# A hybrid attention and retention step on one core: the first transfers laid out and placed anew

## The chip, the cores and the metric

One core of one Trainium2 chip runs the whole program, in one launch. The metric is the device time of that launch in microseconds (us), lower is better; it is given as the median of three runs.

## What is computed

Two groups of tokens, a prompt of 1024 and a sample group of 8 (one new token for each of 8 sequences), pass through two layers: sliding-window attention (32 query heads, 4 key heads, window 128, sinks, a relative-position bias) and retention (4 heads, keys of 256, values of 512), each with a SiLU gate, and a last norm. All in 32-bit floats. Cut to what the change touches:

```python
logits = einsum('bqkgd,bskd->bkgqs', q, k) * 64 ** -0.5
bias = rel_bias[t5_bucket(rel)]            # rel = query position - key position
logits = where(valid, logits + bias, -1e30)
m = maximum(max(logits), sink); p = exp(logits - m)
o = einsum('bkgqs,bskd->bqkgd', p / (sum(p) + exp(sink - m)), v)
...
kb = concatenate([cache_k, k_new], axis=1)  # sample group: 128 cached rows and the new one
vb = concatenate([cache_v, v_new], axis=1)
return y, kb[:, 1:], vb[:, 1:]              # the cache moved on by one row
...
q, k = rotary(q, pos), rotary(k, pos)       # retention: cos and sin tables by position
```

## The kernel before

Tokens lie along the free dimension in two halves of 512; the 8 sample tokens ride with the first half, so its width is 520 (`TA`). Nearly all the work is products against weights. Each weight tile is 128 x 512 (256 KB) and is split into a high and a low part, `whi` and `wlo`, so that three products (high by high, high by low, low by high) give nearly full precision. `wload` (L170) does this: SP issues the load into `wraw` (3 buffers), ACT casts it to `whi` (4 buffers), and GpSimd and VectorE take turns to subtract for `wlo` (4 buffers). So a load is issued when the tile three before it has been split, and that needs the buffers of a tile that TensorE has finished. A feature tile of an input projection takes two weight tiles; each weight tile is 24 products of 260 columns (`proj_job`, L347: two column chunks of 12).

The order. Only TensorE's instructions stand in the order in which the code is written (`MANUAL`, L53). Those of the other engines, and the transfers that SP issues, are placed by a scheduler, which estimates times and puts an instruction early where what it needs is there early. Each engine then runs its own list in order. All transfers of the kernel are issued by SP, in one list: when one has to wait, for a buffer, for data, or in its issue, all behind it wait.

The first stretch. The first half's stream is loaded and split as it arrives (`first_x`, L1088), beside the four weight tiles of the value projection (`w_v`, tiles 1 to 4). Then come the two key tiles of features (`k_job`: weight tiles 5 to 8), the first queries (9 to 12) and the first gates (13 to 16), all of `w_in`. `bias_rows` (L441) loads the small tables; after four pieces of the stream (weight tiles 5 and 6) TensorE multiplies the bias table `rb` by the one-hot table `hot` into `bps`, ACT copies this to `brow`, one row of 128 per head, and four transfers (L457) write each row 128 times into DRAM tiles `bdram`. `att_scores` (L608) reads them back with a step of 127 (L613), so that every row is the bias turned by one: one `bias` tile of four heads, a read before each group of four blocks. The first such read stands right behind the four writes.

The attention loop runs 64 slots (L1164): in each slot scores of one tile, turns of the one before, values of the one before that; jobs of the stream are spread between. `extra` hangs further stages on slots: at slot 3 `move_cache` (L709), which moves the sample caches on by one row from DRAM to DRAM, 1016 KB each; at slots 8u + 3, 5 and 7 `att_sample(u)` (L666), the sample group's eight heads: it loads cached keys `kT` (L671), cached values `vc` (L673, rows 1 to 127 on 127 partitions), the new token's value row (L674, from `vsmp` into partition 0), the bias rows `bs` (L679). `load_rope(0)` (L717), hung on slot 56, loads the cos and sin tables that retention reads at L735 and L745. As the scheduler put them, the cache moves, `kT`, `vc` and the rope loads of the first half stand on SP ahead of the sixth weight tile.

Of the kernel before, what the change touches and what calls it, by code (L numbers as in the profile page):

```python
# [10 lines left out]
F32 = mybir.dt.float32  # L11
# [8 lines left out]
P = 128  # L20
# [3 lines left out]
NB = 8  # L24
# [9 lines left out]
# columns of the constant tensor  # L34
# [13 lines left out]
# weight tiles loaded ahead of their use; the slack in spreading the stream, in ns of  # L48
# the tensor engine; products that bring it to its full clock while the first loads come
# [10 lines left out]
class Stream:  # L60
    """The matrix products against the weights, as jobs in their order. A job is a
    generator that yields after each piece with the piece's length on the tensor
    engine; its weight tiles are loaded some tiles ahead of their use."""
# [21 lines left out]
    def step(self):  # L85
        """one piece of the first job; True when the job is over."""
        j = self.jobs[0]
        if j[1] is None:
            j[1] = j[0]()
        try:  # L90
            j[2] -= next(j[1])
            return False
        except StopIteration:
            self.jobs.pop(0)
            return True

    def fill(self, n, goal):
        """the first n jobs until about goal of them is left; how many of them are left."""
# [12 lines left out]
def hybrid_step(ctx: ExitStack, tc: tile.TileContext, I: dict, O: dict):  # L111
# [17 lines left out]
    # ---- token halves: the sample tokens ride with the first half, except in  # L129
    # the last output projection, where they ride with the second  # L130
# [6 lines left out]
    # ---- the residual stream: one half on chip at a time, the other in DRAM  # L137
# [30 lines left out]
    wctr = [0]  # L168

    def wload(src):  # L170
        raw = wp.tile([P, 512], F32, name="wraw", tag="wr", bufs=3)
        sp.dma_start(raw, src)
# [10 lines left out]
    # ================= norms =================  # L183
    H = [None]

    def stats_rows(s, T):
        """the reciprocal root mean squares, with tokens on partitions, from the squares' sums over tiles."""
# [13 lines left out]
    def stats_spread(rs, T, tag):  # L201
        """the same, with tokens along the row, on every partition."""
# [16 lines left out]
    def norm_stats(T, tag, out, stored=None):  # L219
        """out: the reciprocal root mean square of each token, on every partition; in three stages."""  # L220
# [19 lines left out]
    def norm(layer, T, rb_, src):  # L240
        """the normalised half, split in two parts; src(kt, tile) is the stream's tile. In four stages."""
# [32 lines left out]
    def final_norm(hf, T):  # L274
        """in four stages."""
# [8 lines left out]
    def final_part(c0, c1):  # L284
        """the last norm of columns c0..c1 of the second half, in four stages."""
# [54 lines left out]
    # ================= projections =================  # L340
# [6 lines left out]
    def proj_job(src, evac):  # L347
        """one feature tile of an input projection: evac(psum, c0, c1) per column chunk."""
# [18 lines left out]
    def tok_job(srcs, width, smp, evac):  # L367
        """a projection with tokens on partitions: evac(block, psum); block 4 is the
        sample rows, whose two parts lie on partitions 0.. and 32.. and are to be added."""
# [33 lines left out]
    def out_job(T, src, ys, fts):  # L403
        """feature tiles of an output projection, added to the stream."""
# [27 lines left out]
    # ================= attention layer =================  # L432
# [4 lines left out]
    bdram = [dp.tile([8, P, P], F32, name=f"bdram{u}") for u in range(4)]  # L437
# [3 lines left out]
    def bias_rows():  # L441
        """relative-position bias: one row per head, repeated over its period, kept in DRAM."""
# [11 lines left out]
        brow = lp.tile([HEADS, P], F32, name="brow")  # L454
        act.copy(brow, bps[:HEADS, :P])
        for u in range(4):
            sp.dma_start(bdram[u], brow[8 * u : 8 * u + 8, None, :].to_broadcast([8, P, P]))  # L457
            yield
# [82 lines left out]
    def q_jobs(m):  # L541
        """queries of four heads, in the two parts that the tensor engine takes, one above the other."""
# [65 lines left out]
    def att_scores(i):  # L608
        m, b = i // 4, i % 4
        hf, u, t = m // 8, (m // 2) % 4, m % 2  # L610
        if b == 0:
            bi = lp.tile([P, 4, P], F32, name="bias", tag="bias", bufs=2)
            sp.dma_start(bi, bass.AP(bdram[u].tensor, bdram[u].offset + 4 * t * P * P, [[P - 1, P], [P * P, 4], [1, P]]))  # L613
# [731 lines left out]
```

## Time and profile before

| what | value |
|---|---|
| runs | 1785.62, 1788.95, 1789.3 us; median 1788.95 |
| profiled execution, first to last instruction (span) | 1782.7 us |
| what lies around it, against the median (the profiled execution's time is given by its span alone) | 6.25 us |
| TensorE granted clock, mean over the span | 0.981 |
| DMA | 211.30 MB, mean 119 GB/s |
| TensorE waits for its weight tile's first part | 36.1 us, in 2 places |

Times are microseconds from the first instruction. Engines: PE is TensorE, PEld its weight load, DVE is VectorE, ACT ScalarE, POOL GpSimd, SPq the queue of transfers that SyncE issues. A row of a timeline has the start, the length, the engine, the line of the kernel, the operation, what it writes and reads, and in brackets how long the engine had been idle and what released it. For SPq the length is that of the issue, not of the transfer. A row of stretches has, for each engine, its busy time and in brackets how many instructions, then the granted clock (1.00 is full), the busy share of the 16 DMA engines, and GB/s. A row of DMA issues has the number, the size of one, and the median time from issue to landing.

### The profile page before, as it was taken

The page shows a single profiled execution, that of the slowest core. Times are in us where ns is not written, and L with a number is a line of the kernel's source. Part 1 is how long each engine was busy: PE and PEld are TensorE (multiplying, and loading weights), DVE is VectorE, ACT ScalarE, POOL GpSimd, SP SyncE. Part 2 cuts the span into 40 slices and gives each one's busy share as a digit, 9 for nine tenths or more (in the row PEclk, how much of TensorE's full clock was granted, in tenths as well). Part 3 has the DMA queues.
Part 4 walks back from the last instruction along what each step waited for, and adds up shares of the span by engine and source line. Part 5 has one row for each costly group of instructions (what it writes and reads, how often), then busy time and mean ns, then how long its engine had stood idle before and what let it go on. Part 6 is the DMA issues. An engine that isn't in the chain of part 4 may idle for free.

```text
span 1782.7 us, 29003 instructions
## 1 busy us (share of the span) xinstructions
PE 1705.9 (96%) x10550; PEld 1454.3 (82%) x10550; DVE 1049.3 (59%) x2142; ACT 842.2 (47%) x1960; POOL 709.5 (40%) x670
## 2 busy tenths in 40 slices
PE   6489999999999999999999999999999999999997
PEld 6488999898888777778889788787777889888887
DVE  4367767776467666675276465456655655445366
ACT  4255646455555555565354344344443433433344
POOL 2024443445334434344434334234344452443534
PEclk8789999999999999999999999999999999999999
DMA  5432224223234222232366456447454262322323
GB/s 179 81 92 67 89 78 118 85 88 108 88 113 150 83 83 77 77 90 72 107 204 209 144 155 211 149 136 243 136 179 152 66 201 73 99 83 77 109 64 125
DMA packets 127442, 211.30 MB, mean 119 GB/s; under 512 B 17036, under 2 KB 32004, under 8 KB 127268
## 3 DMA queue, kind: packets, MB, share of 16 engines
q1 hardware_dynamic: 127300, 209.46, 38.4%
q8 instruction: 83, 1.36, 0.3%
q14 instruction: 59, 0.48, 0.1%
HBM read 177.56 MB, written 33.91 MB: 119 GB/s over the span
## 4 chain that ended last, share of the span: by engine, by line
PE 83%; DVE 4%; DMA 2%; ACT 1%; POOL 1%; issue 1%; SPq 0%; POOLq 0%; DVEq 0%; ACTq 0%
PE gemm L358 13%; PE gemm L359 12%; PE gemm L360 12%; PE gemm L385 3%; PE gemm L386 3%; PE gemm L387 3%; PE gemm L413 3%; PE o L663 3%; PE gemm L1061 3%; PE gemm L1059 3%; PE gemm L1060 3%; PE gemm L414 3%; PE gemm L415 3%; PE S L624 3%; PE pt L641 1%
## 5 line engine op out<-in xcount | busy, mean ns | idle before, releaser
L358 PE MATMUL gemm<-hh,whi 128*128 128x260 f32 (+1 forms) x1584 | 523.8, 331 | 36.1 <-ACT whi L174 36.1
L178 POOL TENSOR_TENSOR wlo<-wraw,whi 128x512 fp32r<-128x512 f32 x236 | 310.1, 1314 | 599.0 <-ACT whi L174 580.7
L174 ACT CAST whi<-wraw 128x512 fp32r<-128x512 f32 x472 | 290.8, 617 | 485.3 <-PE gemm L359 142.5
L360 PE MATMUL gemm<-hh,wlo 128*128 128x260 f32 (+1 forms) x1584 | 508.8, 321 | 0.5 <-POOL wlo L178 0.5
L359 PE MATMUL gemm<-hl,whi 128*128 128x260 f32 (+1 forms) x1584 | 508.7, 321 | 0.0
L358 PEld LDWEIGHTS gemm<-hh,whi 128*128 128x128 f32 x1584 | 300.8, 190 | 82.1 <-ACT whi L174 41.8
L360 PEld LDWEIGHTS gemm<-hh,wlo 128*128 128x128 f32 x1584 | 300.6, 190 | 23.8 <-POOL wlo L178 0.8
L359 PEld LDWEIGHTS gemm<-hl,whi 128*128 128x128 f32 x1584 | 301.0, 190 | 20.2 <-issue 0.5
L178 DVE TENSOR_TENSOR wlo<-wraw,whi 128x512 fp32r<-128x512 f32 x236 | 196.0, 831 | 206.1 <-ACT whi L174 203.0
L430 POOL TENSOR_TENSOR yl<-yf,yh 128x256 fp32r<-128x256 f32 x128 | 106.9, 844 | 97.8 <-ACT yh L429 97.4
L413 PE MATMUL gemm<-yh,whi 128*128 128x260 f32 (+1 forms) x384 | 127.1, 331 | 5.0 <-DVE xa L417 5.0
L385 PE MATMUL gemm<-whi,hh 128*128 128x512 f32 (+1 forms) x320 | 122.3, 382 | 3.1 <-DVE ra L745 3.1
L1059 PE MATMUL gemm<-yh,whi 128*128 128x260 f32 (+3 forms) x384 | 124.7, 325 | 0.0
L414 PE MATMUL gemm<-yl,whi 128*128 128x260 f32 (+1 forms) x384 | 123.5, 322 | 0.0
L415 PE MATMUL gemm<-yh,wlo 128*128 128x260 f32 (+1 forms) x384 | 123.5, 322 | 0.0
L1060 PE MATMUL gemm<-yl,whi 128*128 128x260 f32 (+3 forms) x384 | 122.8, 320 | 0.0
L1061 PE MATMUL gemm<-yh,wlo 128*128 128x260 f32 (+3 forms) x384 | 122.8, 320 | 0.0
L598 ACT ACTIVATE L<-L,nm 128x128 f32<-128x128 f32 x256 | 99.8, 391 | 48.3 <-DVE nm L593 48.0
L387 PE MATMUL gemm<-whi,hl 128*128 128x512 f32 (+1 forms) x320 | 119.3, 373 | 3.3 <-DVE hl L1096 3.2
L386 PE MATMUL gemm<-wlo,hh 128*128 128x512 f32 (+1 forms) x320 | 119.5, 373 | 0.0
L602 POOL TENSOR_TENSOR L<-L,rsum 128x512 f32<-128x512 f32 x64 | 75.9, 1185 | 83.5 <-DVE rsum L601 48.0
L413 PEld LDWEIGHTS gemm<-yh,whi 128*128 128x128 f32 x384 | 72.8, 190 | 16.2 <-issue 8.7
(246 smaller groups left out, 3137.0 us busy)
## 6 DMA issues: line engine op xcount, KB each, us to landing
wraw<-in_w_in SPq DMA_DIRECT2D x264, 256.0 KB, 2.6
wraw<-in_w_out SPq DMA_DIRECT2D x136, 256.0 KB, 2.6
wraw<-in_w_v SPq DMA_DIRECT2D x72, 256.0 KB, 2.6
Rsm<-in_state SPq DMA_DIRECT2D x64, 256.0 KB, 4.2
out_ret_state_sample<-Rsm SPq DMA_DIRECT2D x64, 256.0 KB, 3.4
vrow<-vdram SPq DMA_DIRECT2D x32, 256.0 KB, 3.8
bias<-bdram SPq DMA_DIRECT2D x16, 256.0 KB, 2.9
xdram<-xa SPq DMA_DIRECT2D x16, 256.0 KB, 2.4
```

What stands on the lines that cost most here:

```text
L174: act.copy(hi, raw)
L178: eng.tensor_tensor(out=lo, in0=raw, in1=r32(hi), op=ALU.subtract)
L358: pe.matmul(ps, a, hh[k][:, c0:c1], start=(k == 0), stop=False)
L359: pe.matmul(ps, a, hl[k][:, c0:c1], start=False, stop=False)
L360: pe.matmul(ps, b, hh[k][:, c0:c1], start=False, stop=(k == KT - 1))
L385: pe.matmul(ps, hh[k][:, cs], wh, start=(k == 0), stop=False)
L413: pe.matmul(ps, a, yh[:, k % 2, c0:c1], start=(k == 0), stop=False)
L414: pe.matmul(ps, a, yl[:, k % 2, c0:c1], start=False, stop=False)
L415: pe.matmul(ps, b, yh[:, k % 2, c0:c1], start=False, stop=(k == 3))
L1059: pe.matmul(ps, a, yh[:, k % 2, c0:c1], start=(k == 0), stop=False)
L1060: pe.matmul(ps, a, yl[:, k % 2, c0:c1], start=False, stop=False)
L1061: pe.matmul(ps, b, yh[:, k % 2, c0:c1], start=False, stop=(k == 3))
```

## The change

There are four edits. The bias: `brow` now holds each head's row 8 times (ACT copies with a repeat), and one transfer writes it 16 times per head into one DRAM tensor `bdram`, 2 MB as before, in 512 pieces of 4 KB in place of 4096 of 512 bytes; the readers address this tensor. The cache moves: the same bytes, each as 16 runs of 2032 elements for every sequence, with the 16 as the outermost dimension (before, the 8 sequences were), and at slot 12 in place of 3. The sample values: `vc` is loaded on all 128 partitions, with partition 0 overwritten by the new row afterwards (before, rows 1 to 127 alone). And the cache moves, all stages of `att_sample` and `load_rope(0)` are traced inside `issue_after`, which keeps what they issue on SP behind the weight load that was traced last. As `move_cache` has left slot 3, the first sample stage there is traced one piece of the stream earlier.

```diff
     def wload(src):
         raw = wp.tile([P, 512], F32, name="wraw", tag="wr", bufs=3)
-        sp.dma_start(raw, src)
+        last[0] = sp.dma_start(raw, src)
...
-    bdram = [dp.tile([8, P, P], F32, name=f"bdram{u}") for u in range(4)]
+    bdram = dp.tile([HEADS, 16, 8 * P], F32, name="bdram")
...
-        brow = lp.tile([HEADS, P], F32, name="brow")
-        act.copy(brow, bps[:HEADS, :P])
-        for u in range(4):
-            sp.dma_start(bdram[u], brow[8 * u : 8 * u + 8, None, :].to_broadcast([8, P, P]))
-            yield
+        brow = lp.tile([HEADS, 8, P], F32, name="brow")
+        act.copy(brow, bps[:HEADS, None, :P].to_broadcast([HEADS, 8, P]))
+        sp.dma_start(bdram, brow.rearrange("h a t -> h (a t)")[:, None, :].to_broadcast([HEADS, 16, 8 * P]))
+        yield
...
-            sp.dma_start(bi, bass.AP(bdram[u].tensor, bdram[u].offset + 4 * t * P * P, [[P - 1, P], [P * P, 4], [1, P]]))
+            sp.dma_start(bi, bass.AP(bdram.tensor, bdram.offset + (8 * u + 4 * t) * P * P, [[P - 1, P], [P * P, 4], [1, P]]))
...
-        sp.dma_start(vc[1:P], I["cache_v"][:, 1:P, 64 * u : 64 * u + 64].rearrange("b w d -> w b d"))
+        sp.dma_start(vc, I["cache_v"][:, :, 64 * u : 64 * u + 64].rearrange("b w d -> w b d"))
         sp.dma_start(vc[0:1], vsmp[:, 64 * u : 64 * u + 64])
...
-            sp.dma_start(bs[8 * b2 : 8 * b2 + 8], bdram[u][:, 0, :])
+            sp.dma_start(bs[8 * b2 : 8 * b2 + 8], bdram[8 * u : 8 * u + 8, 0, 0:P])
...
+        n = (WIN - 1) * 256 // 16
         for nm in ("k", "v"):
-            sp.dma_start(O[f"swa_{nm}_sample"][:, 0 : WIN - 1, :], I[f"cache_{nm}"][:, 1:WIN, :])
+            o, i = O[f"swa_{nm}_sample"], I[f"cache_{nm}"]
+            dims = [[n, 16], [WIN * 256, NB], [1, n]]
+            sp.dma_start(bass.AP(o.tensor, o.offset, dims), bass.AP(i.tensor, i.offset + 256, dims))
...
-    many((2, 4, 6), bias)
-    at(3, move_cache)
+    def behind_weights(fn):
+        def run():
+            with tc.issue_after(last[0].ins):
+                return fn()
+        return run
+
+    at(12, behind_weights(move_cache))
     for u in range(4):
-        many((8 * u + 3, 8 * u + 5, 8 * u + 7), att_sample(u))
+        for i, f in zip((3, 5, 7), [behind_weights(stager(att_sample(u)))] * 3):
+            at(8 * u + i, f)
...
     at(41, swap_a)
-    at(56, lambda: load_rope(0))
+    at(56, behind_weights(lambda: load_rope(0)))
```

How this moves instructions is shown at two places. On SP in the kernel before, from the fifth weight tile (the first `wraw<-in_w_in`) to the first bias read:

```order
L172 DMA wraw<-in_w_in 128x512
L445 DMA sink_s<-in_sinks_s 16x4
L448 DMA rb<-in_rel_bias 32x32
L712 DMA out_swa_k_sample<-in_cache_k 8x2x16256
L712 DMA out_swa_v_sample<-in_cache_v 8x2x16256
L671 DMA kT<-in_cache_kT 128x512
L673 DMA vc<-in_cache_v 127x8x64
L721 DMA cos<-in_rope 128x520
L172 DMA wraw<-in_w_in 128x512
L722 DMA sin<-in_rope 128x520
L172 DMA wraw<-in_w_in 128x512 x2
```

The same stretch of SP in the changed kernel, as far as the two bias reads:

```order
L173 DMA wraw<-in_w_in 128x512
L446 DMA sink_s<-in_sinks_s 16x4
L449 DMA rb<-in_rel_bias 32x32
L173 DMA wraw<-in_w_in 128x512 x5
L451 DMA hot<-in_hot 32x128
L173 DMA wraw<-in_w_in 128x512
L535 DMA out_swa_v_sample<-vsmp 8x256
L173 DMA wraw<-in_w_in 128x512
L457 DMA bdram<-brow 512x1x1024
L173 DMA wraw<-in_w_in 128x512 x3
L613 DMA bias<-bdram 128x4x128 x2
```

The two cache moves, `kT`, `vc` and both rope loads have left this place; weight tiles 6 to 10 follow the fifth. The bias write stands after tile 12, three weight loads behind it, and then the reads that need it. Before, the four writes stood after tile 12 as well, with the first read right behind them. `kT`, `vc` and `bs` of the first sample group now come after tile 24, the cache moves after tile 46, the rope loads after tile 186.

On VectorE in the kernel before, at the end of the first stretch (`sq` is the sum of squares, `nps` the row of statistics that TensorE makes of it, `rs` what becomes of that):

```order
L1098 CAST hs<-hl_338 128x8
L1111 TENSOR_TENSOR sq_161<-sq_161,sq_171 128x520
L197 TENSOR_SCALAR rs<-nps 128x5
L204 TENSOR_TENSOR dg<-cst,rs 128x512
L208 TENSOR_SCALAR dg<-cst,rs 8x8
```

And in the changed kernel:

```order
L1101 CAST hs<-hl_335 128x8
L179 TENSOR_TENSOR wlo<-wraw,whi 128x512
L1114 TENSOR_TENSOR sq_158<-sq_158,sq_168 128x520
L198 TENSOR_SCALAR rs<-nps 128x5
L205 TENSOR_TENSOR dg<-cst,rs 128x512
L209 TENSOR_SCALAR dg<-cst,rs 8x8
```

A weight tile's low part (tile 6) has moved ahead of the last sum of squares.

More of the change, by code (lines that the diff above doesn't have):

```diff
@@ L168, in hybrid_step @@
     wctr = [0]
+    last = [None]
     def wload(src):
         raw = wp.tile([P, 512], F32, name="wraw", tag="wr", bufs=3)
-        sp.dma_start(raw, src)
+        last[0] = sp.dma_start(raw, src)
         hi = wp.tile([P, 512], F32R, name="whi", tag="wh", bufs=4)
```

## The prediction

> **What bounds the kernel now.** First the page: how long, and which engine is busy.
>
> ```profile
> span 1782.7 us, 29003 instructions
> PE 1705.9 (96%) x10550; PEld 1454.3 (82%) x10550; DVE 1049.3 (59%) x2142; ACT 842.2 (47%) x1960; POOL 709.5 (40%) x670
> PE   6489999999999999999999999999999999999997
> PEclk8789999999999999999999999999999999999999
> ```
>
> The tensor engine is the bound nearly everywhere; only the first three slices (44.6 us each) hold holes, and there the granted clock is low too. So a change of first transfers is worth what those slices lose. Next the list of PE's waits (us in total, times, longest):
>
> ```profile
> PE gemm L358 <- ACT whi L174: 36.1, 2, 26.0
> PE pt L641 <- POOL L L602: 9.2, 4, 3.3
> ```
>
> The first entry is the large one; its two places in PE's timeline (start, length, what, idle before):
>
> ```profile
> 40.63 0.58 PE L358 MATMUL gemm<-hh,whi 128*128 128x260 f32 x1 [10.07 <-ACT whi L174]
> ...
> 90.56 0.59 PE L358 MATMUL gemm<-hh,whi 128*128 128x260 f32 x1 [26.04 <-ACT whi L174]
> ```
>
> Two waits, 10.07 and 26.04 us, both for a weight tile's first part. ACT's timeline says that its cast waited for a weight load:
>
> ```profile
> 39.96 0.62 ACT L174 CAST whi<-wraw 128x512 fp32r<-128x512 f32 x1 [12.48 <-DMA wraw<-in_w_in]
> 89.89 1.26 ACT L174 CAST whi<-wraw 128x512 fp32r<-128x512 f32 x2 [29.44 <-DMA wraw<-in_w_in]
> ```
>
> Why were the loads late? SP issues every transfer of this kernel, in one queue. Its timeline (start, length of the issue):
>
> ```profile
> 10.91 0.90 SPq L712 DMA_DIRECT2D out_swa_k_sample<-in_cache_k  x1
> ...
> 13.07 0.39 SPq L673 DMA_DIRECT2D vc<-in_cache_v  x1
> 13.50 23.14 SPq L721 DMA_DIRECT2D cos<-in_rope  x1
> 36.75 0.36 SPq L172 DMA_DIRECT2D wraw<-in_w_in  x1
> ...
> 47.36 28.18 SPq L457 DMA_DIRECT2D bdram<-brow  x4
> 75.58 7.64 SPq L613 DMA_DIRECT2D bias<-bdram  x1
> 83.33 3.96 SPq L172 DMA_DIRECT2D wraw<-in_w_in  x2
> ```
>
> SP stood 23.14 us in the rope load, behind the cache shift and the sample values, and the second weight tile of the input projection (36.75) came only after it. Then the four bias writes and the first bias read (which waits until they have landed) held it from 47.36 to 83.22, 35.9 us, with weights behind. How fast things moved, and at which clock PE resumed (columns: PE, PEld, DVE, ACT, POOL, clock, DMA share, GB/s):
>
> ```profile
> 40.00:50.00 10.00, 9.37 (x51) 8.54 (x52) 5.62 (x12) 7.29 (x17) 2.55 (x2) 0.65 0.54 171
> 50.00:60.00 10.00, 10.00 (x85) 10.00 (x85) 8.79 (x24) 4.97 (x12) 1.29 (x1) 1.00 0.38 44
> 90.00:100.00 10.00, 8.89 (x46) 8.59 (x47) 7.60 (x15) 5.62 (x13) 3.97 (x3) 0.59 0.51 153
> 100.00:110.00 10.00, 10.00 (x86) 9.95 (x86) 3.78 (x8) 4.54 (x7) 1.93 (x2) 1.00 0.39 106
> ```
>
> After each hole PE ran at about half clock for a while. At full clock 86 products take 10 us, 0.116 us each, 2.79 us for a weight tile's 24. So the 51 products of 40 to 50 needed 5.93 us and took 9.37: 3.44 lost. The 46 of 90 to 100 needed 5.35 and took 8.89: 3.54 lost.
>
> **What goes.** 10.07 + 26.04 + 3.44 + 3.54 = 43.1 us, if nothing else is late there.
>
> The first hole: by the order of SP's instructions the shift, kT, vc and both rope loads no longer stand ahead of the weights; after the fifth weight tile follow five more in a row, each as its buffer comes free. Nothing is then between PE at 26.04 and the tiles it wants. That part is bounded by the 10.07 + 3.44 that it costs now.
>
> The second hole hangs on one price, the new bias write. PE's order is nearly untouched (the first sample's four score products come one piece earlier), so PE starts the fifth tile at 26.04, ends the sixth two tiles later, 31.6, and the bias product follows. A weight cast (0.62) and the bias copy, eight times wider now, come next on ACT. Two rows bound that copy:
>
> ```profile
> 47.08 0.26 ACT L455 COPY brow<-bps 32x128 f32<-32x128 f32 x1
> 108.38 1.07 ACT L583 ACTIVATE g<-g 128x1040 f32<-128x1040 f32 x1
> ```
>
> I take 1.07 (1024 elements per row, like the second). With some 0.3 for hand-overs, and 0.7 that the next part adds, the write is issued at 34.3. By then twelve weight tiles have been issued; tiles 13, 14, 15 stand behind it in the queue, and after them the bias read, which blocks SP until the write has landed. PE reaches tile 13 at 26.04 + 0.7 + 8 x 2.79 = 49.1. Less the cast (0.62) and some 0.1, tile 13 must land by 48.4, so the write may take 14.1 us before PE waits. Its bounds:
>
> ```profile
> out_ret_state_prompt<-R SPq DMA_DIRECT2D x4, 512.0 KB, 2.8
> 8.00:10.00 2.00, 1.83 (x15) 1.83 (x16) 1.93 (x7) 2.00 (x4) 0.00 (x0) 1.00 1.04 394
> ```
>
> At the best rate seen, 394 GB/s, 2.10 MB take 5.3 us; at the old writes' pace, 35.9. The nearest row is the prompt-state store: the same direction, the same 4 KB pieces, 512 KB landed 2.8 us after issue. Four of these are 11.2 us, and I take that: landed at 45.5, 2.9 us to spare, cost nothing. The weights behind the bias read are issued late, but tile 16 is wanted only at 57.5, twelve microseconds on; the first scores need the bias after the last first-phase weight tile, near 60.
>
> That 50-60 row moves 44 GB/s at a DMA share of 0.38, with little but bias writes in flight. [...]
>
> **What is added or moved besides.** On DVE a weight tile's second part now stands ahead of the last sum of squares, for whose result PE's statistics wait:
>
> ```profile
> 22.08 0.69 DVE L1111 TENSOR_TENSOR sq<-sq,sq 128x520 f32<-128x520 f32 x1
> 40.61 0.69 DVE L178 TENSOR_TENSOR wlo<-wraw,whi 128x512 fp32r<-128x512 f32 x1 [12.32 <-ACT whi L174]
> 22.95 0.95 PE L193 MATMUL nps<-ones,sq 128*128 128x1 f32 x8
> ```
>
> The sum ends at 22.77 and PE goes on at 22.95, so 0.69 more on DVE lies on the path: 0.7 lost.
>
> The sample loads (kT, values, bias rows), four times, and the shift, once, now stand between weights. What cover weights have there, this trace shows at the second sample group:
>
> ```profile
> 174.14 0.28 SPq L673 DMA_DIRECT2D vc<-in_cache_v  x1
> 174.47 14.52 SPq L674 DMA_DIRECT2D vc<-vsmp  x1
> ...
> 189.58 1.40 SPq L172 DMA_DIRECT2D wraw<-in_w_in  x3
> ```
>
> A weight load's time to landing, all four waits of that kind, and one stretch of that hold (columns as above):
>
> ```profile
> wraw<-in_w_in SPq DMA_DIRECT2D x264, 256.0 KB, 2.6
> L674 SPq DMA_DIRECT2D vc<-vsmp x4: 713/14298/14518, 39.5 to 363.1; - x4
> 180.00:185.00 5.00, 5.00 (x45) 5.00 (x44) 3.32 (x6) 3.40 (x5) 2.74 (x4) 1.00 0.08 18
> ```
>
> From 174.47 on SP issued no weight until 189.58, and that one needed 2.6 more: some 17.7 us, and PE was busy throughout (5.00 of 5.00). So a hold of up to 17.7 us costs nothing there. It also means that taking out the later holds behind the sample values (median 14.3; 127 partitions now 128) gains nothing: I count 0 for them. Their cover is this reserve of loaded tiles; without it each would cost its length.
>
> The shift, 2.08 MB: with the values' load (14.5 us, by the row above) it was through when the rope issue ended, 36.64, that is 25.7 us after 10.91, so it took at most 11.2, and on no more than that again now: below 17.7, so 0. A gain is excluded too, as nothing waits for its output. The one new wait is that the new token's value row overwrites part of the now whole values' tile, and so waits for that load; behind it in SP's queue stand weights, and the load is of the size that lands in 2.6 to 3: 0, by the same cover. The rope tables, two loads of 260 KB (some 5 us at 2.6 each), go past 181 weight loads, to before the last bias read of the attention layer, which is issued at 748:
>
> ```profile
> L613 SPq DMA_DIRECT2D bias<-bdram x16: 377/377/7644, 75.6 to 748.3; - x16
> L735 DVE TENSOR_TENSOR rf<-gemm,cos x24: 414/429/692, 851.6 to 1674.0; 128x260 f32<-128x260 f32 x16, 128x512 f32<-128x512 f32 x8
> ```
>
> They are first read at 851.6, a hundred later: 0. The wider bias copy (0.8 on ACT) is in the write's issue time already, and what follows it on ACT has tile 6's PSUM, which PE needs back two tiles later.
>
> **The sum.** 1782.7 - 43.1 + 0.7 = 1740.3 us of span. The median of the runs, 1788.95, is 6.25 above the span (1785.62 to 1789.3: 2.9 to 6.6). 1740.3 + 6.25 = 1746.5.
>
> **The rivals.** A, the bias write still opens a hole. For it: 32 partitions instead of 128 may feed it more slowly than the store that I priced it by. Against: its pieces are eight times longer than the old ones. With half the old time, 18 us, tile 13 lands at 34.3 + 18 + 0.6 = 52.9, PE waits from 49.1 to 53.6, 4.5 us, and if that is enough to halve the clock as before, 3.5 more: 1754.5. It decides at 14.1 us.
>
> B, the write is not changed in what counts, and takes its 35.9 again. For it: the bytes are the same 2.10 MB, and the DMA share of the old writes was only 0.38, so something other than the engines may have held them. Then tile 13 lands at 70.8, PE goes on at 71.5, 22.4 late, and 3.5 for the clock: 1772.4. Only the first hole would be gone, and part of the second.
>
> C, slower than before: the shift, moved to stand between weights 46 and 47, takes longer in its new runs than the cover and the gain together, 17.7 + 42.4 + 3.6 = 63.7 us. For it: the stretch 180 to 185 shows how slow small pieces can be, 18 GB/s with the sample values alone in flight; 2.08 MB at that pace are 115.6 us, and PE would lose 115.6 - 17.7 + 3.5 = 101: 1848. Against: the pieces are of 8 KB, not 256 bytes, and the old shift did at least 2.08 MB in 11.2 us, 186 GB/s. It decides below 33 GB/s.
>
> **How the numbers follow.** Forecast, both holes gone: 0.76. A 0.14, B 0.05, C 0.02; 0.02 for a still lower time, where other waits shrink with the new order; 0.01 for holes that merely move and leave the time. The time is the forecast's, 1746.5. Its own bounds: down by the 0.7 of DVE and by 3.3, as far as the lowest run lies under the median, with 2 of the 9.2 us that PE waits for attention weights (the second wait quoted), which may fall better: 1740.5. Upward A's 1754.5 and 2 for those same waits falling worse: 1756.5. B, C and the still lower time stay outside, 0.10 in all. A measurement of this kernel tells about 0.2%, 3.6 us, from no change; only C (0.02) is slower, holes that merely move (0.01) are no change, and the rest is faster: 0.97.
>
> **What would show it.** In the profile after: PE's waits hold no entry for a weight cast above a few us; the clock stays full from 10 to 100 us; the first slices of PE read 9; SP's rope issue is short and near 700 us; the bias write lands within 14 us of its issue and the bias read's issue ends there; the first score exponentials come some 42 us earlier. A PE wait of 4 us or more near 49 would be A, of 20 or more B; a wait near 190 behind the shift would be C. The prediction is also wrong if the holes go and the time does not fall by some 42: then something that these holes covered, such as a tile's attention weights, is late instead.

## The result, and the profile after

| | before | changed |
|---|---|---|
| median of the runs | 1787.5 us (1785.62 to 1789.3, 4 runs) | 1738.91 us (1736.35 to 1741.44, 4 runs) |
| ratio, 95% interval | | 0.9725 (0.9705 to 0.9746) |
| profiled execution: span | 1782.7 us | 1734.6 us (whole time 1736.38) |

The changed kernel is faster by 48.6 us between the medians, and by 48.1 between the two spans. The forecast was 1746.5, 7.6 too high, and the result lies 1.6 under the low end of the range, 1740.5. The direction and the two holes were foretold; the range was not wide enough downward.

The page after, in the lines that were shown of before:

```profile
span 1734.6 us, 29003 instructions
PE 1697.7 (98%) x10550; PEld 1450.0 (84%) x10550; DVE 1045.5 (60%) x2142; ACT 841.1 (48%) x1960; POOL 713.2 (41%) x670
PE   9999999999999999999999999999999999999997
PEclk9999999999999999999999999999999999999998
```

The first three slices of PE, 6, 4 and 8 before, read 9, and so does its clock. The list of PE's waits after: the entry for a weight cast, 36.1 us before, is gone, and the wait for attention weights leads.

```profile
PE pt L641 <- POOL L L602: 7.9, 5, 2.5
PE gemm L414 <- DVE xa L418: 4.4, 2, 2.9
```

SP's timeline after shows why (start, length of the issue):

```profile
13.14 11.18 SPq L173 DMA_DIRECT2D wraw<-in_w_in  x5
...
37.25 0.68 SPq L457 DMA_DIRECT2D bdram<-brow  x1
38.02 7.22 SPq L173 DMA_DIRECT2D wraw<-in_w_in  x3
49.63 0.94 SPq L613 DMA_DIRECT2D bias<-bdram  x2
...
76.72 0.77 SPq L674 DMA_DIRECT2D vc<-vsmp  x1
```

Where the rope load stood for 23.14 us, five weight tiles go out. The bias write is issued at 37.25 (34.3 was foretold), and the first bias read goes at 49.63: 12.4 us against the 11.2 of the forecast. That is under the 14.1 at which PE was to wait, and yet there was nothing to spare. PE came to tile 13 at 52.49 (foretold: 49.1), and waited there for the tile's low part:

```profile
53.28 0.39 PE L361 MATMUL gemm<-hh,wlo 128*128 128x260 f32 x1 [0.39 <-POOL wlo L179]
```

The value row's transfer, 14.5 us of hold before, takes 0.77. Two stretches of the changed kernel (PE, PEld, DVE, ACT, POOL, clock, DMA share, GB/s):

```profile
20.00:30.00 10.00, 9.54 (x56) 8.18 (x54) 5.19 (x14) 3.28 (x7) 2.92 (x3) 0.79 0.39 111
...
40.00:48.00 8.00, 8.00 (x69) 8.00 (x68) 6.93 (x17) 3.95 (x10) 1.06 (x1) 1.00 0.96 199
```

From 40 to 48 the DMA packets are, but for a few, the write's pieces of 4 KB: they move at 199 GB/s, where 44 went in the 50 to 60 of before, and PE works at full clock. The weights issued behind the write move after it. The 0.79 in 20 to 30 comes from two half-clock stretches, near 17 and 24 us, where before has none: the forecast's sign of a full clock from 10 to 100 failed there. Of the two repeats of the changed kernel one has both and one has neither, so they are chance.

**Where the 48.1 came from.** TensorE runs its 10,550 products in nearly the same order in both kernels, so the start times of the same product can be laid side by side. The table gives the time that PE took from one product's start to another's (in the last row, to the start of the last product), in two profiled executions of before and three of the changed kernel (the first of each are the ones above; the others are repeats, told below).

| products | before | before again | changed | changed again | changed, third |
|---|---|---|---|---|---|
| 0 to 380 (both holes) | 97.7 | 96.5 | 56.4 | 55.6 | 57.0 |
| 380 to 1000 | 81.6 | 83.0 | 79.5 | 79.5 | 79.5 |
| 1000 to 2000 | 119.9 | 120.2 | 119.8 | 119.8 | 119.8 |
| 2000 to 2950 | 121.9 | 126.1 | 119.8 | 121.4 | 119.8 |
| 2950 to 7000 | 681.8 | 681.7 | 681.4 | 681.9 | 681.5 |
| 7000 to 8200 | 227.3 | 228.0 | 224.3 | 223.7 | 223.7 |
| 8200 to the end | 443.6 | 444.1 | 444.7 | 443.6 | 445.1 |

The first row gives 41.3, where the forecast counted 42.4. The other 6.7 us come from behind the holes, in three places where the forecast counted nothing: products 380 to 1000, 2000 to 2950 and 7000 to 8200. PE's timeline of before at the first two of them, with the idle time in brackets:

```profile
135.63 1.11 PE L641 MATMUL pt<-cst,L 128*128 128x128 f32 x4 [2.97 <-POOL L L602]
136.67 0.61 PE L688 MATMUL ss<-kT,qbd 128*16 128x128 f32 x2
...
314.22 0.36 PE L413 MATMUL gemm<-yh,whi 128*128 128x260 f32 x1 [2.74 <-DVE xa L417]
```

The same places in the changed kernel:

```profile
89.89 1.05 PE L688 MATMUL ss<-kT,qbd 128*16 128x128 f32 x8
94.36 0.66 PE L641 MATMUL pt<-cst,L 128*128 128x128 f32 x4 [1.76 <-POOL L L602]
...
269.34 0.36 PE L414 MATMUL gemm<-yh,whi 128*128 128x260 f32 x1 [1.48 <-DVE xa L418]
```

At the first place nothing became quicker: the attention weights come at the end of the same chain. But the eight products of the first sample's scores (`ss`, 1.05 us), which had run behind the wait, now run before it, and fill 1.2 of its 2.97 us. And the shorter wait leaves the clock alone. Before, behind that wait and behind the two waits of the second place, near 314 and 411 (the one near 314 left the clock alone in this execution):

```profile
135.00:140.00 5.00, 4.37 (x22) 3.26 (x23) 3.60 (x8) 1.09 (x4) 1.30 (x3) 0.66 0.44 110
313.00:318.00 5.00, 3.78 (x29) 3.14 (x30) 4.16 (x16) 2.87 (x14) 1.27 (x1) 1.00 0.39 111
411.00:416.00 5.00, 4.86 (x25) 3.52 (x26) 5.00 (x12) 2.73 (x4) 2.49 (x2) 0.66 0.50 147
```

After, behind the first:

```profile
94.00:99.00 5.00, 4.64 (x37) 3.98 (x38) 4.90 (x11) 2.41 (x9) 2.27 (x4) 1.00 0.42 105
```

A mean clock of 0.66 over 5 us means about 3.4 us at half clock (in the first of these rows the clock is 0.50 from 135.7 to 139.0 us), which costs up to 1.7 us when PE has work throughout. In all, the clock record of before holds 4 such stretches behind the holes (near 136, 412, 805 and 1242), that of before again 8 (counting each of two of double length as two); the three executions of the changed kernel hold 1, 2 and 1. Three stretches fewer, one in each of the three places, are up to 5.1 of the 6.7 us, and the shorter waits are most of the rest.

### The profile page after: what moved, and what is told of

Read it like the earlier page. It is cut to its first block, busy times and chain, and to the rows that moved or that the text cites. A ratio compares the mean times of both kernels' runs of the same rounds, so it can differ in the third digit from the quotient of the medians.

```text
span 1734.6 us, 29003 instructions
## 1 busy us (share of the span) xinstructions
PE 1697.7 (98%) x10550; PEld 1450.0 (84%) x10550; DVE 1045.5 (60%) x2142; ACT 841.1 (48%) x1960; POOL 713.2 (41%) x670
## 4 chain that ended last, share of the span: by engine, by line
PE 81%; DVE 5%; DMA 3%; ACT 2%; POOL 2%; issue 1%; SPq 0%; POOLq 0%; ACTq 0%; DVEq 0%
PE gemm L359 12%; PE gemm L360 12%; PE gemm L361 12%; PE gemm L386 4%; PE gemm L387 3%; PE gemm L388 3%; PE o L663 3%; PE gemm L1063 3%; PE gemm L1062 3%; PE gemm L1064 3%; PE gemm L414 3%; PE gemm L416 3%; PE gemm L415 3%; PE S L624 3%; PE pt L641 1%
## 5 line engine op out<-in xcount | busy, mean ns | idle before, releaser
L179 DVE TENSOR_TENSOR wlo<-wraw,whi 128x512 fp32r<-128x512 f32 x236 | 190.1, 806 | 161.6 <-ACT whi L175 159.5
```

Of the source, the lines that this page charges most:

```text
L179: eng.tensor_tensor(out=lo, in0=raw, in1=r32(hi), op=ALU.subtract)
```

## The experiments

Times are medians, and ratios are to the kernel before, run beside each on the same chip.

**The bias write alone**, in the kernel before:

```diff
-    bdram = [dp.tile([8, P, P], F32, name=f"bdram{u}") for u in range(4)]
+    bdram = dp.tile([HEADS, 16, 8 * P], F32, name="bdram")
...
-        act.copy(brow, bps[:HEADS, :P])
-        for u in range(4):
-            sp.dma_start(bdram[u], brow[8 * u : 8 * u + 8, None, :].to_broadcast([8, P, P]))
+        act.copy(brow, bps[:HEADS, None, :P].to_broadcast([HEADS, 8, P]))
+        sp.dma_start(bdram, brow.rearrange("h a t -> h (a t)")[:, None, :].to_broadcast([HEADS, 16, 8 * P]))
```

> The kernel before with the bias edit alone (one write of 4 KB pieces; shift, sample values and rope as before). Theory, two holes with separate causes: the wait of about 10 us for a weight cast stays, the one of 26 us goes with its half clock; span 1782.7 - 29.5 = 1753, median near 1758. Rival, the bias write only fits because the other loads have left: tile 13 then comes late and a hole of 5 to 10 us opens in place of the second one, median 1765 to 1770.

Measured: 1756.34 us, ratio 0.9833 (0.9811 to 0.9855). PE's waits and SP's timeline of this kernel:

```profile
PE gemm L358 <- ACT whi L174: 10.6, 1, 10.6
```

```profile
47.80 0.69 SPq L456 DMA_DIRECT2D bdram<-brow  x1
...
60.20 0.39 SPq L612 DMA_DIRECT2D bias<-bdram  x1
```

One wait of 10.6 is left, the first hole; the second has gone. The write takes 12.4 us here too. So the write's new shape alone takes the second hole away.

**The placing alone**: in the kernel before, the cache shift at slot 12, and the shift, the sample stages and the rope loads each behind the last weight load; all shapes old.

```diff
-        sp.dma_start(raw, src)
+        last[0] = sp.dma_start(raw, src)
...
-    at(3, move_cache)
+    at(12, behind_weights(move_cache))
...
-    at(56, lambda: load_rope(0))
+    at(56, behind_weights(lambda: load_rope(0)))
```

> The kernel before with the placing alone (shift, sample and rope loads behind weights; all transfers in their old shapes). Theory: the first hole (13.3 us with the clock) goes; the four old bias writes still stand ahead of tiles 13 to 15 and of the first bias read, so a hole of some 20 to 25 us stays, in one or two pieces: span 1760 to 1770. The 127-partition value loads hold SP for 14 us four times in the attention loop and cost nothing. Rival, the placing is what counts: within 5 us of the changed kernel, 1739.

Measured: 1791.83 us over 10 runs, ratio 1.0033 (1.002 to 1.0045). Placing alone makes the kernel slower than before, by 0.3%, which no theory foresaw. By the table's measure the first stretch won 13.7 us (97.7 to 84.0), and products 2000 to 2950 lost 18.9 (121.9 to 140.8). The 13.7 are the first hole: PE's two waits for a weight cast here, 24.2 in all, stand at tiles 13 and 14, among the old bias writes. Why the loss, in three views of this kernel: PE's waits, SP, and what ACT and PE did then.

```profile
PE gemm L359 <- ACT whi L175: 24.2, 2, 13.8
PE ss L689 <- ACT ptp L648: 16.1, 3, 8.1
```

```profile
276.93 14.52 SPq L675 DMA_DIRECT2D vc<-vsmp  x1
291.49 0.92 SPq L229 DMA_DIRECT2D sqb<-in_x  x2
```

```profile
294.33 0.63 ACT L230 ACTIVATE sqb<-sqb 128x512 f32<-128x512 f32 x1 [13.25 <-DMA sqb<-in_x]
...
298.33 0.59 ACT L648 COPY ptp<-pt 128x512 f32<-128x512 f32 x1 [0.17 <-DVE ptc L644]
```

```profile
298.97 1.89 PE L689 MATMUL ss<-kT,qbd 128*16 128x128 f32 x8 [6.48 <-ACT ptp L648]
```

Read them in this order. The values' load on 127 partitions holds SP for 14.52 us. At its old place it stood ahead of weight loads, of which several tiles were in reserve. Now the second half's stream (`sqb`) stands right behind it. ACT's next instruction in order squares that stream, so ACT stands 13.25 us; the copy of the attention weights is queued behind on ACT, and PE waits 6.48 for it. It happens again near 406, for 8.08.

**The placing with the values on 128 partitions**: the kernel just told, and one edit.

```diff
-        sp.dma_start(vc[1:P], I["cache_v"][:, 1:P, 64 * u : 64 * u + 64].rearrange("b w d -> w b d"))
+        sp.dma_start(vc, I["cache_v"][:, :, 64 * u : 64 * u + 64].rearrange("b w d -> w b d"))
```

> The placing with one new shape, the sample values on 128 partitions; the shift and the bias writes in their old shape. It tells what the placing alone lost in the attention loop, where PE waited three times some 5 to 8 us before the sample scores. Theory, the 14.5 us in which SP waits for the 127-partition load, now directly ahead of the bias rows and of the second half's stream: these three waits and their half clocks go, 25 to 30 us less than the placing alone: median 1762 to 1767; the holes of the four bias writes (24 us) stay. Rival, it is the placing itself, whatever the shape: near 1792.

Measured: 1768.95 us, ratio 0.9903 (0.9885 to 0.992): 23 us under the kernel just told. Products 2000 to 2950 take 120.0 in place of 140.8, and PE waits for `ptp` no more. So the loss was the 127-partition load, and its price depends on what stands behind it.

**The shapes of shift and values alone**, at their old places and with the old bias writes:

```diff
-            sp.dma_start(O[f"swa_{nm}_sample"][:, 0 : WIN - 1, :], I[f"cache_{nm}"][:, 1:WIN, :])
+            o, i = O[f"swa_{nm}_sample"], I[f"cache_{nm}"]
+            dims = [[n, 16], [WIN * 256, NB], [1, n]]
+            sp.dma_start(bass.AP(o.tensor, o.offset, dims), bass.AP(i.tensor, i.offset + 256, dims))
```

> The kernel before with the new shapes of the cache shift (16 runs) and of the sample values (128 partitions), everything in its old place and the bias writes as before. Theory, SP was blocked by how long these two took and not by where they stood: the 23 us issue of the rope load shrinks below 1, tile 6 lands before PE needs it at 28, the first hole goes: span 1769, median 1774; the second hole stays near 26. Rival, the place counts: 2 MB ahead of tile 6 still make PE wait 5 us or more.

Measured: 1767.78 us, ratio 0.9901 (0.9874 to 0.9927). SP's rope issue and PE's waits of this kernel:

```profile
13.60 4.63 SPq L724 DMA_DIRECT2D cos<-in_rope  x1
```

```profile
PE gemm L358 <- ACT whi L174: 26.2, 1, 26.2
```

The rope load still stands ahead of the weights, but holds SP for 4.63 us instead of 23.14, and only the second hole is left. To take the first hole away the shapes are enough; nothing had to be moved. Which of the two shapes counts more was not run apart, but a stretch of before within the 23.14 us speaks:

```profile
24.00:36.00 12.00, 6.55 (x45) 5.33 (x44) 1.95 (x5) 1.94 (x5) 1.54 (x2) 0.89 0.08 18
```

These are the 0.08 and 18 GB/s of 180 to 185, where the values' load on 127 partitions was alone in flight. So at least 12 of the 23.14 us were that load, and not the shift.

**The changed kernel without the placing** (all the new shapes, all at the old places):

```diff
-    at(12, behind_weights(move_cache))
+    at(3, move_cache)
...
-    at(56, behind_weights(lambda: load_rope(0)))
+    at(56, lambda: load_rope(0))
```

> The changed kernel without the placing: new shapes and the new bias write, shift, sample and rope loads in their old place ahead of the weights. Theory: both holes gone as in the changed kernel, median 1736 to 1742; if anything 0.7 less, as VectorE keeps its old order at the statistics. Rival, the placing is needed for the first hole: 10 to 13 us above the changed kernel, near 1750.

Measured: 1735.28 us (1733.54 to 1739.45), ratio 0.9718 (0.9694 to 0.9743): no difference from the changed kernel can be told. What the placing gives at the first attention wait it takes elsewhere. This kernel at that wait:

```profile
91.85 0.66 PE L641 MATMUL pt<-cst,L 128*128 128x128 f32 x4 [2.95 <-POOL L L602]
```

```profile
92.00:97.00 5.00, 5.00 (x29) 4.15 (x29) 3.20 (x9) 2.53 (x10) 0.73 (x2) 0.66 0.57 154
```

Without the placing the sample's products come behind the wait again, it is 2.95 long, a half-clock stretch follows, and products 380 to 1000 take 81.8 instead of 79.5. But the first 380 take 54.0 instead of 55.6 to 57.0, and 2000 to 2950 take 118.7 instead of 119.8 to 121.4 (PE's second wait for `xa` there is 1.73 us, and 2.95 to 2.97 in the three executions of the changed kernel).

**The bias write twice**: the changed kernel with a second copy of the write ahead of the first, into a tile that nobody reads.

```diff
+    bdram_b = dp.tile([HEADS, 16, 8 * P], F32, name="bdram_b")
...
+        sp.dma_start(bdram_b, brow.rearrange("h a t -> h (a t)")[:, None, :].to_broadcast([HEADS, 16, 8 * P]))
         sp.dma_start(bdram, brow.rearrange("h a t -> h (a t)")[:, None, :].to_broadcast([HEADS, 16, 8 * P]))
```

> The changed kernel with a second copy of the bias write, to a tensor that nobody reads, ahead of the real one: 4.2 MB in place of 2.1. Theory (tiles 13 to 15 stand behind the write, PE has a reserve of tiles until about 51): tile 13 lands near 37.3 + 24.6 = 62, PE waits some 10 to 11 us and loses 3.5 more to the clock: 13 to 15 us above the changed kernel, and the bias read is issued near 62. Rival, the reserve is deeper or the writes overlap with the weights: less than 4 us.

Measured: 1751.96 us, ratio 0.9811 (0.9789 to 0.9833), 13.0 us above the changed kernel's median, and 15.9 above its one run on the same chip. PE's waits and SP's timeline:

```profile
PE gemm L359 <- ACT whi L175: 9.5, 1, 9.5
```

```profile
36.18 0.68 SPq L458 DMA_DIRECT2D bdram_b<-brow  x1
36.91 0.61 SPq L459 DMA_DIRECT2D bdram<-brow  x1
...
59.69 0.94 SPq L615 DMA_DIRECT2D bias<-bdram  x2
```

The two writes take 22.8 us, past the 14.1 of the forecast's bound by 8.7; PE waits 9.5, and the clock is halved for 7.0 us behind that, which costs up to 3.5 more. That is rival A's mechanism with its price, on a kernel in which it does happen.

**The bias write from 128 partitions**: each head's row on four partitions of `brow`, each written 4 times.

```diff
-        brow = lp.tile([HEADS, 8, P], F32, name="brow")
-        sp.dma_start(bdram, brow.rearrange("h a t -> h (a t)")[:, None, :].to_broadcast([HEADS, 16, 8 * P]))
+        brow = lp.tile([P, 8, P], F32, name="brow")
+        sp.dma_start(
+            bdram.rearrange("h (c r) x -> (h c) r x", c=4),
+            brow.rearrange("h a t -> h (a t)")[:, None, :].to_broadcast([P, 4, 8 * P]))
```

> The changed kernel with the bias write fed from all 128 partitions (each head's row on 4 of them, each written 4 times), bytes and pieces as in the changed kernel. [...] The time does not change by more than the spread of runs, since no one waits for it.

One run: 1734.3 us, span 1732.6. SP's timeline:

```profile
36.24 0.65 SPq L459 DMA_DIRECT2D bdram<-brow  x1
...
44.33 0.99 SPq L617 DMA_DIRECT2D bias<-bdram  x2
```

8.1 us from the write's issue to the read's, where 32 partitions need 12.4. But here the read no longer waits for the write: it goes right behind the third weight load, which had waited for its buffer until 43.9. So 8.1 is only an upper bound for the write. Its rate is seen in a stretch in which only its 4 KB pieces move, to be set beside the 199 GB/s of the changed kernel:

```profile
38.00:42.00 4.00, 4.00 (x36) 4.00 (x35) 3.44 (x9) 1.97 (x6) 1.39 (x1) 1.00 1.04 401
```

With four times the partitions the same bytes, in pieces of the same size, move at twice the rate, 401 GB/s against 199: the partitions count. How much the longer pieces did for the rate beside the partitions, from 8 to 32 in one transfer, no run separates.

**All the shapes, the write from 128 partitions, no placing**, beside the changed kernel a third time:

> The new shapes in their old places (no placing) and the bias write fed from 128 partitions: the two variants that stood lowest, together. Theory: nothing waits for what either saves beyond the changed kernel, so 1733 to 1738, at most 3 below the changed kernel on the same chip, which the runs may not tell from it. Rival, the placing has a value of its own that the one look did not show: 3 or more above.

> The changed kernel beside the last one, on the same chip: 1736 to 1741.

Measured: 1737.58 us (1736.09 to 1740.46), ratio 0.9726 (0.971 to 0.9743), and the changed kernel 1737.3 (1736.58 to 1741.2), ratio 0.9727 (0.971 to 0.9744). A quicker write can save PE no more than its 0.39 us at tile 13, and that these runs cannot tell. None of the kernels that were tried beats the changed one by more than can be told.

**Tile 6 on GpSimd**: the changed kernel, and the low part of the sixth weight tile, which stands ahead of the last sum of squares on VectorE, given to GpSimd.

```diff
-        eng = pool if wctr[0] % 2 else vec
+        eng = pool if wctr[0] % 2 or wctr[0] == 6 else vec
```

> The changed kernel with the low part of weight tile 6 made on GpSimd in place of VectorE, so that it no longer stands ahead of the last sum of squares. Theory: the 0.7 us that the prediction counted (1.4 at the half clock seen there) come back: the fifth weight tile starts 0.7 to 1.4 earlier, and the time is lower by that, too little for the runs to tell. Rival: the start of the fifth tile is set by something else there (the values' PSUM), and does not move.

Measured: 1744.17 us (1742.66 to 1745.46), ratio 0.9765 (0.9737 to 0.9793): slower than every run of the changed kernel, by 5 us in the median, where a gain of about one was expected. One line of the scheduler's input moved more than one instruction. The timeline of this kernel:

```profile
19.59 1.22 DVE L1101 CAST hs<-hl 128x8 fp32r<-128x8 f32 x1
...
28.04 0.62 ACT L175 CAST whi<-wraw 128x512 fp32r<-128x512 f32 x1 [4.98 <-PE vsp L390]
...
29.07 0.84 ACT L528 ACTIVATE vb<-gemm,rs 128x256 f32<-128x256 f32 x2
...
29.60 0.58 PE L359 MATMUL gemm<-hh,whi 128*128 128x260 f32 x1 [1.38 <-ACT vb L528]
```

The same instructions in the changed kernel's timeline:

```profile
19.09 0.16 DVE L1101 CAST hs<-hl 128x8 fp32r<-128x8 f32 x1
...
25.57 1.69 ACT L528 ACTIVATE vb<-gemm,rs 128x256 f32<-128x256 f32 x4 [3.05 <-POOL rs L199]
27.42 0.62 ACT L175 CAST whi<-wraw 128x512 fp32r<-128x512 f32 x1 [0.17 <-PE vsp L390]
```

A weight cast has moved ahead of the values' evacuation on ACT (`vb`, 25.57 in one and 29.07 in the other), and PE waits 1.38 us for that. So the edit tells nothing of the 0.7 that it was to test, except that it costs more to put right this way than to leave. Some 3.4 us of its loss are in the first 380 products (59.8 against 56.4) and the rest in small steps later, which were not followed up.

**Both kernels again**, one run each:

> The changed kernel again, for a second trace. If the gain beyond the 42.4 of the forecast comes from the new order, its steps (2.6 near the first sample scores, 0.8 to 2.3 at three later places) stand in this trace too; if they are chance of the clock's windows, some are missing and others are there, and the time lies at either 1736 or 1741 as in the four runs.

> The kernel before again, for a second trace. The two holes (10 and 26 us) are there in the same places. If the gain beyond the holes (6.7 us of the 48.1 between the two spans, in steps near 137, 314, 412, 805 and 1242 us of the first trace) is a matter of single runs, this trace has its half-clock windows elsewhere, and against it the changed kernel's gain behind the holes differs by 2 us or more from 6.7. If it belongs to the order, the same steps stand here.

Measured: the changed kernel 1736.1 us, span 1734.4; before 1790.1, span 1788.3. These two profiles of the changed kernel agree to 0.2 us in span (its four runs spread over 5.1); those of before differ by 5.6, and the table shows 4.2 of that in products 2000 to 2950. Behind one and the same wait near 1305 (2.48 us, for `ktl`) stands, in the first profile of before:

```profile
1303.00:1308.00 5.00, 4.42 (x25) 3.04 (x26) 0.75 (x4) 2.12 (x4) 0.45 (x1) 1.00 0.44 143
```

and in the second:

```profile
1307.00:1312.00 5.00, 4.82 (x18) 3.09 (x19) 0.48 (x4) 2.19 (x3) 0.05 (x1) 0.66 0.51 153
```

The same wait, and once the clock is halved after it and once not. It stands in all fourteen traces, at 2.47 or 2.48 us, and six of them have a half-clock stretch behind it. So part of a difference between two single profiles is chance, in steps of at most 1.7 us.

## Why the prediction was wrong, point by point

**The holes: right.** The forecast gave 43.1 us for the two waits and the half clock behind them, less 0.7 at the start; the first 380 products took 41.3 less in the first pair of profiles. The bias-only kernel and the shapes-only kernel each show one of the two holes alone, and the doubled write shows that the hole comes back with a longer write, at the price of rival A. The bound of 14.1 us was too high: it let tile 13 land together with the write. But the tile's own load moves after the write (its cast starts at 51.24, 1.6 us after the bias read is issued), and PE needs the low part as well, which is made after the cast. PE waits 0.39 us at a write of 12.4, and 9.5 at one of 22.8, so the waiting starts near 12 to 13. The write and PE's arrival at tile 13 were both some 3 us later than foretold, which about cancels. That the price of 11.2 came near the 12.4 was luck as well: the row that it was taken from stores from 128 partitions and, by its packets, in pieces of 2 KB and not of 4. Rivals B and C did not happen: the write is not as slow as before, and PE stays busy during the shift.

**The failed step: "taking out the later holds behind the sample values (median 14.3; 127 partitions now 128) gains nothing: I count 0 for them".** It rested on one stretch of PE, 180 to 185, with 5.00 of 5.00 busy. That row is true, and says what the second hold costs while it lasts, and in weights. It says nothing of what is late tens of microseconds on. The bias-only kernel and the changed kernel without placing differ by the shapes of shift and values alone, and the shift is through in the first 24 us: behind product 380 they take 1680.0 and 1671.5, 8.5 us apart, and 7.3 of these are in products 2000 to 2950. PE's waits there, first with the old shapes, then with the new:

```profile
284.92 0.42 PE L413 MATMUL gemm<-yh,whi 128*128 128x260 f32 x1 [2.70 <-DVE xa L417]
...
384.67 0.56 PE L413 MATMUL gemm<-yh,whi 128*128 128x260 f32 x1 [3.56 <-DVE xa L417]
```

```profile
269.42 0.36 PE L414 MATMUL gemm<-yh,whi 128*128 128x260 f32 x1 [1.67 <-DVE xa L418]
...
365.82 0.36 PE L414 MATMUL gemm<-yh,whi 128*128 128x260 f32 x1 [1.73 <-DVE xa L418]
```

The two waits are 1.03 and 1.83 longer with the hold, and the clock record has three half-clock stretches of 3.4 us behind them that are not there without it: 2.9 + 3 x 1.7 = 8.0 at most, where 7.3 were found. The way from the hold to the wait is the one that the placing alone shows large: the stream's loads are queued behind it. Counted from PE's product 2000, the last of the eight loads of the stream (`sqb`) is issued at 6.6 to 6.8 us in the three traces with the old load at its old place, and at 5.4 to 5.5 in the three with the new one; the first sum into `xa` behind it, which stands on VectorE among the squares of that stream, starts at 13.2 to 13.6 and at 12.2. PE's two waits for `xa` come to 5.0, 6.7 and 6.3 us with the old load, and to 3.3 or 3.4 with the new one. In the first profile of before this term was only 2.1 of the 6.7, in part because of the chance in the clock; in the second it was 6.3.

**A second term missed: the score products.** The forecast noted that the first sample's products (four, it said; the trace has eight) come one piece earlier, and gave it no price. At a wait of 2.97 us, what the program does just before or just behind is worth its length: 1.2 us, and mostly the half-clock stretch as well (the longer wait, 2.94 to 2.97 us, has one behind it in five of six traces, the shorter, 1.76 to 1.79, in none of seven). The row with that wait was summed in the quoted 9.2 us of PE's waits for attention weights, of which the low bound took 2. The changed kernel without the placing loses it again (2.95, clock 0.66), so this is shown.

**The sum's last step, "1740.3 + 6.25".** The 6.25 was the median of the runs less one span, taken as what lies around a span. What lies around it is 1736.38 - 1734.6 = 1.8 us in the run of the changed kernel. The other 4.5 say that the profiled execution of before, about 1784.5, was a quick one, below all the runs shown. For the changed kernel the same difference is 1738.91 - 1734.6 = 4.3. So of the 7.6 us by which the forecast was high, 1.9 are this step, and 5.7 the span (1740.3 against 1734.6): 6.7 from behind the holes, less 1.1 at them.

**The range.** Its low end took 3.3 for the runs' scatter and 2 for the attention waits falling better. With the gain behind the holes, 6.7 to 13.6 by which execution of before it is measured from, it would have had to reach some 5 us lower: that is 6.7 where it took 2 for other waits. (The chances outside, B, C and the still lower time, sum to 0.09; the 0.10 has the holes that merely move in it.)

**What was credited to the wrong edit.** The forecast gave the first hole to the new order on SP. That order does remove it, but so do the shapes alone, and the order alone, with the old values' load, makes the kernel slower as a whole. With all the shapes in place, no gain from the order can be told. A forecast of the whole can come near the result without knowing this.

**Open.** Products 7000 to 8200 take 3 to 4 us less in the changed kernel than in before. There PE waits for retention's sum (`osum`) for 2.4 and 2.6 us in the two profiles of before, and 1.4 to 1.6 in those of the changed kernel; with the bias write alone it is 1.5, with the shapes alone 2.0, without the placing 1.8. That fits no single edit. The clock fits better: the six traces without a half-clock stretch in these products take 223.5 to 224.8 us, the eight with one or two take 226.2 to 228.0, and the shapes without the placing are once among the first (224.8, with the write from 128 partitions) and once among the second (226.4). So at least part of these 3 to 4 us is chance; whether the shorter waits for `osum` make the stretches rarer was not settled.

## What to carry to other kernels

A transfer that blocks an issuing queue costs what is queued behind it, and not what it takes: the same 14.5 us were worth nothing to a few microseconds ahead of weights in reserve, and about ten ahead of a load that an in-order engine consumes next (18.9 us in products 2000 to 2950 of the placing alone, with two such holds). So mend a transfer's shape before moving it, and judge a hold by following each thing behind it to its reader, not by whether the bound engine is busy during it. And where the gain is a few per cent, take two profiled executions before building a sum on one: this kernel's differ by 5.6 us.

## What the runs showed of the hardware that was not expected

- Half-clock stretches of about 3.4 us (3.41 in the clock record, from 135.66 us of the first profile of before), some of double length, came with waits of 1.8 to 3.6 us of a PE that is otherwise busy, and did not come with the same wait each time: the wait of 2.48 us near 1305 had one behind it in six of fourteen traces. The stretch near 24 us in the first profile of the changed kernel came with no wait above 0.36 us since the stretch before it. What decides whether the clock is halved was not shown.
- 2 MB from 8, 32 and 128 partitions into DRAM took 35.9 (four writes in a row, pieces of 512 bytes), 12.4 and at most 8.1 us (pieces of 4 KB), from the issue to that of the read that waits for it; while little but the write moved, the rates were 44, 199 and 401 GB/s.
- The value row's transfer, which waits for the values' load, took 14.2 to 14.5 us to issue right behind the load on 127 partitions (three of the four in before; the fourth came after the rope load's 23.14 us and took 0.71). With the load on 128 partitions it took 0.68 to 0.77 (the four in the changed kernel), issued 4.8 to 5.0 us after the load. During the hold the DMA share was 0.08, at 18 GB/s (180 to 185 us of before). Why one partition less makes the load so slow was not shown.
- A cast of 128 x 8 on VectorE (`hs<-hl`) took 1.22 us while GpSimd was in a subtract of 128 x 512, and 0.16 in the kernel where it was not. It ended 0.02 us after that subtract. Two later casts of this kind are as slow in every trace (0.88 to 0.90 and 1.28 to 1.30 us, ending within 0.05 us of GpSimd's instruction). None of the 166 casts in all traces without a GpSimd instruction beside them took more than 0.17; of the 58 with one, half were as quick.
